# A 3x3 convolution plus residual: a rolled TensorE loop over four images, one weight load per four matmuls, hand-made semaphores, weights on another queue

## The chip, the cores and the metric

The kernel runs on one core of one Trainium2 chip. The metric is the device time of one execution in microseconds; lower is better. The four runs of the kernel before lie within 0.23 us (0.2%). "Span" is the length of the one profiled execution as the trace sees it; it is shorter than the time (123.3 us against 125.16 for the profiled run of the changed kernel).

## The reference

```python
batch, c_in, h, w, c_out, k = 16, 64, 64, 64, 64, 3      # all float32
x_pad = np.pad(x, ((0, 0), (0, 0), (1, 1), (1, 1)))
for b, co, ci, kh, kw in ...:
    output[b, co] += weight[co, ci, kh, kw] * x_pad[b, ci, kh:kh+h, kw:kw+w]
return output + residual
```

x, residual and output are 16.8 MB each, so at least 50.3 MB have to pass between HBM and the core; the page of the kernel before counts 33.70 MB read and 16.78 written.

## The kernel before

The images are taken in pairs: a pair of x is one 2 MB load over 128 partitions, and so are a pair of residuals and a pair of outputs. The chain of one image is: load x; cast it to bf16 and rearrange it so that even and odd rows lie on different partitions ("pack", on ScalarE, the first two images partly on VectorE); 24 matmuls of 512 or 504 columns into one of two PSUM tiles; two VectorE additions of the residual; after the second image of a pair, the store. All waits and semaphores are placed by the framework. The cuts are marked with dots.

```python
    xr = [pool.tile([128, NPIX], FP32, name=f"xr{i}") for i in range(NXR)]     # 3 raw pairs of x
    xp = [pool.tile([128, J + 1, W], BF16, name=f"xp{i}") for i in range(4)]   # 4 packed images
    ...
    def convolve(n):
        t = xp[n % 4]
        ps = psum.tile([128, NCHUNK, JC, W], FP32, name="ps")
        order = [(1, 0), (1, 1), (0, 0), (0, 1), (2, 0), (2, 1)]
        for i, (kw, d) in enumerate(order):
            ...
            for c in range(NCHUNK):                                            # 4 chunks
                nc.tensor.matmul(out=ps[:, c, :, xlo:xhi], lhsT=wl[:, d, kw, :, :]..., rhs=t[...], ...)
        return ps
    ...
    with tc.manual_schedule():
        nc.gpsimd.dma_start(out=wdup[:, 0, :], in_=w_flat[:, :])               # weights
        ...
        for p in range(NXR):
            load_x(p)
            load_ro(p)
        ...                                        # 9 transposes and 6 copies make wl
        pack(0)
        pack(1)
        for n in range(B):                         # written out: 16 x 24 matmuls, each with its load
            ps = convolve(n)
            if n + 2 < B:
                pack(n + 2)
            ...                                    # every second n: load_x, load_ro of a later pair
            add(n, ps)
            if n >= 9 and n % 2 == 1:
                store((n - 9) // 2)
        for p in range((B - 9) // 2 + 1, NPAIR):
            store(p)
```

Of the kernel before, what the change touches and what calls it, by code (L numbers as in the profile page):

```python
# [1 line left out]

# [5 lines left out]

FP32 = mybir.dt.float32
BF16 = mybir.dt.bfloat16  # L10
ADD = mybir.AluOpType.add


@with_exitstack
def kernel(
    ctx: ExitStack,
    tc: tile.TileContext,
    x: bass.AP,
    weight: bass.AP,
    residual: bass.AP,  # L20
    out: bass.AP,
):
    nc = tc.nc

    B, C, H, W = x.shape
    CO = weight.shape[0]
    K = weight.shape[2]
    assert C == 64 and CO == 64 and K == 3 and H == 64 and W == 64 and B == 16

    NPIX = H * W  # L30
    NPAIR = B // 2
    J = H // 2
    JC = 8
    NCHUNK = J // JC
    NXR = 3

    res_bc = residual.rearrange("b c h w -> (b c) (h w)")
    out_bc = out.rearrange("b c h w -> (b c) (h w)")
    x_bc = x.rearrange("b c h w -> (b c) (h w)")
    w_flat = weight.rearrange("co ci kh kw -> co (ci kh kw)")  # L40

    pool = ctx.enter_context(tc.tile_pool(name="pool", bufs=1))
    psum = ctx.enter_context(tc.tile_pool(name="psum", bufs=2, space=bass.MemoryType.PSUM))

    ident = pool.tile([64, 64], FP32)
    ro = [pool.tile([128, NPIX], FP32, name=f"ro{p}") for p in range(NPAIR)]
    xr = [pool.tile([128, NPIX], FP32, name=f"xr{i}") for i in range(NXR)]

    xp = [pool.tile([128, J + 1, W], BF16, name=f"xp{i}") for i in range(4)]

    wdup = ro[NPAIR - 1][0:64, 0:1152].rearrange("p (d f) -> p d f", d=2)
    wl = pool.tile([128, 2, 3, 2, 64], BF16)

    def load_x(p):
        nc.sync.dma_start(out=xr[p % NXR][:, :], in_=x_bc[128 * p : 128 * p + 128, :])

    def load_ro(p):
        nc.sync.dma_start(out=ro[p][:, :], in_=res_bc[128 * p : 128 * p + 128, :])

    def pack(n):  # L60

        p, im = divmod(n, 2)
        hp = slice(64 * im, 64 * im + 64)
        x4 = xr[p % NXR].rearrange("q (j two w) -> q j two w", two=2, w=W)
        t = xp[n % 4]
        first = nc.vector.tensor_copy if n < 2 else nc.scalar.copy
        first(out=t[64:128, 0:J, :], in_=x4[hp, :, 0, :])  # L67
        nc.scalar.copy(out=t[0:64, 1 : J + 1, :], in_=x4[hp, :, 1, :])  # L68

    def convolve(n):  # L70
        t = xp[n % 4]
        ps = psum.tile([128, NCHUNK, JC, W], FP32, name="ps")
        order = [(1, 0), (1, 1), (0, 0), (0, 1), (2, 0), (2, 1)]
        for i, (kw, d) in enumerate(order):
            xlo, xhi = max(0, 1 - kw), min(W, W + 1 - kw)
            for c in range(NCHUNK):
                j0 = JC * c
                nc.tensor.matmul(  # L78
                    out=ps[:, c, :, xlo:xhi],
                    lhsT=wl[:, d, kw, :, :].rearrange("q r c -> q (r c)"),  # L80
                    rhs=t[:, j0 + d : j0 + d + JC, xlo + kw - 1 : xhi + kw - 1],
                    start=i == 0,
                    stop=i == len(order) - 1,
                    skip_group_check=True,
                )
        return ps

    def add(n, ps):
        p, im = divmod(n, 2)
        hp = slice(64 * im, 64 * im + 64)  # L90
        o4 = ro[p].rearrange("q (j two w) -> q j two w", two=2, w=W)
        psj = ps.rearrange("q c j w -> q (c j) w")
        for par in range(2):
            nc.vector.tensor_tensor(  # L94
                out=o4[hp, :, par, :], in0=psj[64 * par : 64 * par + 64, :, :], in1=o4[hp, :, par, :], op=ADD
            )

    def store(p):
        nc.sync.dma_start(out=out_bc[128 * p : 128 * p + 128, :], in_=ro[p][:, :])


    with tc.manual_schedule():
        nc.gpsimd.dma_start(out=wdup[:, 0, :], in_=w_flat[:, :])  # L103
        make_identity(nc, ident[:, :])
        for p in range(NXR):
            load_x(p)
            load_ro(p)

        for t in xp:
            nc.vector.memset(t[0:64, 0, :], 0.0)  # L110
            nc.vector.memset(t[64:128, J, :], 0.0)  # L111
        nc.vector.memset(wl[0:64, 0, :, 1, :], 0.0)  # L112
        nc.vector.memset(wl[64:128, 1, :, 0, :], 0.0)  # L113


        nc.vector.tensor_copy(out=wdup[:, 1, :], in_=wdup[:, 0, :])  # L116
        wdup3 = wdup.rearrange("p d (ci t) -> p (d ci) t", t=9)
        tp = psum.tile([128, NCHUNK, JC, W], FP32, name="ps")
        for t in range(9):
            nc.tensor.transpose(out=tp[:, t // 8, t % 8, :], in_=wdup3[:, :, t], identity=ident[:, :])  # L120
        tpf = tp.rearrange("p c j w -> p (c j) w")
        for half, d, par, kh in (
            (0, 0, 0, 0),
            (1, 0, 0, 1),
            (1, 0, 1, 0),
            (0, 1, 0, 2),
            (0, 1, 1, 1),
            (1, 1, 1, 2),
        ):
            hp = slice(64 * half, 64 * half + 64)  # L130
            nc.vector.tensor_copy(out=wl[hp, d, :, par, :], in_=tpf[hp, 3 * kh : 3 * kh + 3, :])  # L131

        pack(0)
        pack(1)
        for n in range(B):
            ps = convolve(n)
            if n + 2 < B:
                pack(n + 2)
            p, im = divmod(n, 2)
            if im == 0 and p + NXR < NPAIR:  # L140
                load_x(p + NXR)
                load_ro(p + NXR)
            add(n, ps)
            if n >= 9 and n % 2 == 1:
                store((n - 9) // 2)
        for p in range((B - 9) // 2 + 1, NPAIR):
            store(p)


# [1 line left out]
_INS = ['x', 'weight', 'residual']  # L151
_OUTS = [((16, 64, 64, 64), 'float32')]


# [23 lines left out]
```

## Time and profile before

| | before |
|---|---|
| time, median (range) | 126.01 us (125.88 to 126.11) |
| span | 124.4 us |
| busy share TensorE / VectorE / ScalarE | 69% / 63% / 47% |
| bytes moved, mean rate | 50.53 MB, 406 GB/s |
| weight loads, TensorE | 393 of 99 to 205 ns, beside the matmuls |

The lines that carry the reading are in the prediction below. A transfer of 2 MB is cut into 128 packets of 16 KB, eight for each of the 16 DMA engines, and an engine that is late with one packet is late with all the later ones (in the kernel before, one that lost 1.57 us just after 40.23 us was still 1.56 us behind at the end). The packet records of the trace (start, duration, size, queue) show this; the aggregated views show it only at the very end of the span. The records don't name the DMA engine. Which packets belong to one engine is worked out: the next packet of an engine starts within some 10 ns of the end of the one before, and each engine closes its part of a transfer with a packet of 4 bytes.

### The profile page before, as it was taken

How to read it: one execution, taken by the hardware profiler on the slowest of the kernel's cores; microseconds unless marked ns; L12 is line 12 of the kernel's file. 1: busy time of each engine (PE TensorE's matmuls, PEld its weight loads, DVE VectorE, ACT ScalarE, POOL GpSimd, SP SyncE). 2: the span in 40 equal slices, each digit the busy share in tenths (PEclk: the TensorE clock that was granted, in tenths of full speed). 3: DMA queues.
4: the chain of work that ended last, by engine and by line, in shares of the span. 5: the costliest groups of instructions: out<-in, count | busy, mean ns of one | idle time of the engine just before them, and what ended most of it. 6: DMA issues, size and time to landing. Idle time of an engine off the chain costs nothing.

```text
span 124.4 us, 987 instructions
## 1 busy us (share of the span) xinstructions
PE 86.2 (69%) x386; PEld 39.2 (31%) x393; DVE 79.0 (63%) x51; ACT 58.2 (47%) x31; POOL 1.3 (1%) x7
## 2 busy tenths in 40 slices
PE   0004599999999999999999999999999900000000
PEld 0003134444444444444444444444444300000000
DVE  3015800989889898898988989889898894000000
ACT  4009207966984990896697599399000000000000
POOL 4000000000000000000000000000000000000000
PEclk9999999999999999999999999999999996555555
DMA  5999999999999999999999999999999999999980
GB/s 111 398 324 432 442 427 427 427 432 421 427 421 432 416 432 432 437 432 427 421 421 427 421 421 432 437 432 432 442 421 427 427 421 432 432 437 442 421 369 32
DMA packets 3507, 50.53 MB, mean 406 GB/s; under 512 B 400, under 2 KB 400, under 8 KB 432
## 3 DMA queue, kind: packets, MB, share of 16 engines
q1 hardware_dynamic: 3456, 50.33, 96.2%
q0 software_dynamic: 48, 0.15, 0.3%
q8 instruction: 3, 0.05, 0.2%
HBM read 33.70 MB, written 16.78 MB: 406 GB/s over the span
## 4 chain that ended last, share of the span: by engine, by line
PE 69%; DMA 6%; DVE 5%; DVEq 2%; issue 1%; POOLq 0%
PE ps L78 68%; DMA ro<-in_weight_dram 6%; DVEq L173 2%; DVE ro L94 2%; DVE wl L131 2%; PE ps L120 1%; DVE xp L67 1%; DVE ro L116 0%; POOLq L162 0%; POOLq masks.py:199 0%
## 5 line engine op out<-in xcount | busy, mean ns | idle before, releaser
L78 PE MATMUL ps<-xp,wl 128*128 128x504 bf16 (+1 forms) x377 | 85.0, 387 | 3.6 <-DVE xp L67 3.2
L94 DVE TENSOR_TENSOR ro<-ps,ro 64x2048 f32<-64x2048 f32 x32 | 73.2, 2289 | 15.5 <-PE ps L78 15.3
L78 PEld LDWEIGHTS <-wl 128*128 128x128 bf16 x384 | 38.0, 99 | 50.2 <-DVE xp L67 3.4
L67 ACT CAST xp<-xr 64x2048 bf16<-64x2048 f32 x14 | 26.5, 1896 | 20.6 <-DMA xr<-in_x_dram 20.4
L68 ACT CAST xp<-xr 64x2048 bf16<-64x2048 f32 x16 | 30.4, 1898 | 7.8 <-DMA xr<-in_x_dram 7.4
L120 PE MATMUL ps<-ident,ro 64*128 64x64 f32 x9 | 1.3, 319 | 9.4 <-DVE ro L116 9.4
L116 DVE COPY ro<-ro 64x576 f32<-64x576 f32 x1 | 0.5, 452 | 6.7 <-DMA ro<-in_weight_dram 6.7
L120 PEld LDWEIGHTS ps<-ident,ro 64*128 64x128 f32 x9 | 1.1, 205 | 9.4 <-issue 9.4
L131 DVE CAST wl<-ps 64x192 bf16<-64x192 f32 x6 | 2.0, 352 | 1.5 <-PE ps L120 1.4
L67 DVE CAST xp<-xr 64x2048 bf16<-64x2048 f32 x2 | 2.4, 1219 | 0.0
L68 ACT ACT_TABLE_LOAD x1 | 1.3, 1283 | 0.7 <-PEq L162 0.7
L110 DVE MEMSET xp<- 64x32 uint32 x4 | 0.3, 85 | 1.0 <-PEq L162 0.8
L103 POOL DMA_DIRECT2D ro<-in_weight_dram x1 | 0.6, 644 | 0.8 <-POOLq L162 0.8
L111 DVE MEMSET xp<- 64x32 uint32 x4 | 0.3, 85 | 0.2
masks.py:199 POOL TENSOR_SCALAR_AFFINE_SELECT ident<-ident 64x64 f32<-64x64 f32 x1 | 0.2, 228 | 0.1
L113 DVE MEMSET wl<- 64x96 uint32 x1 | 0.1, 138 | 0.1
L112 DVE MEMSET wl<- 64x96 uint32 x1 | 0.1, 138 | 0.1
masks.py:197 POOL MEMSET ident<- 64x64 f32 x1 | 0.2, 170 | 0.0
L162 POOL MEMSET const-bfloat16-1.0<- 128x1 bf16 x1 | 0.1, 112 | 0.0
L162 POOL MEMSET const-uint8-127<- 128x1 uint8 x1 | 0.1, 112 | 0.0
L162 POOL MEMSET const-float32-0.0<- 128x1 f32 x1 | 0.1, 109 | 0.2 <-issue 0.2
L162 POOL MEMSET const-float32-1.0<- 128x1 f32 x1 | 0.1, 110 | 0.0
## 6 DMA issues: line engine op xcount, KB each, us to landing
xr<-in_x_dram SPq DMA_DIRECT2D x8, 2048.0 KB, 23.1
ro<-in_residual_dram SPq DMA_DIRECT2D x8, 2048.0 KB, 27.6
out_dram<-ro SPq DMA_DIRECT2D x8, 2048.0 KB, 32.7
ro<-in_weight_dram POOLq DMA_DIRECT2D x1, 144.0 KB, 7.6
```

The lines of the kernel that those rows point to most:

```text
L67: first(out=t[64:128, 0:J, :], in_=x4[hp, :, 0, :])
L68: nc.scalar.copy(out=t[0:64, 1 : J + 1, :], in_=x4[hp, :, 1, :])
L78: nc.tensor.matmul(out=ps[:, c, :, xlo:xhi], lhsT=wl[:, d, kw, :, :].rearrange("q r c -> q (r c)"), rhs=t[:, j0 + d : j0 + d + JC, xlo + k ...
L94: nc.vector.tensor_tensor(out=o4[hp, :, par, :], in0=psj[64 * par : 64 * par + 64, :, :], in1=o4[hp, :, par, :], op=ADD)
L103: nc.gpsimd.dma_start(out=wdup[:, 0, :], in_=w_flat[:, :])
L110: nc.vector.memset(t[0:64, 0, :], 0.0)
L111: nc.vector.memset(t[64:128, J, :], 0.0)
L116: nc.vector.tensor_copy(out=wdup[:, 1, :], in_=wdup[:, 0, :])
L120: nc.tensor.transpose(out=tp[:, t // 8, t % 8, :], in_=wdup3[:, :, t], identity=ident[:, :])
L131: nc.vector.tensor_copy(out=wl[hp, d, :, par, :], in_=tpf[hp, 3 * kh : 3 * kh + 3, :])
L162: nc = _bacc.Bacc("TRN2", target_bir_lowering=False, num_devices=1)
L173: with _tile.TileContext(nc) as tc:
```

## The change

The intent is a leaner TensorE: a rolled loop over the four packed tiles in place of 16 written-out images, one weight load for each four matmuls that share weights, and semaphores chosen by hand in one critical section in place of those of the framework. The weights move from GpSimd's queue to ScalarE's ("ACT queue"), and all packs go to ScalarE. The last three stores stand after the section.

```diff
+    def matmul(out_, lhsT, rhs, start, stop, ldweights):
+        if ldweights:
+            return e.matmul(...)
+        return e.add_instruction(mybir.InstMatmult(..., ldweights=False))
...
+    with tc.tile_critical(no_gpsimd_drain=True):
+        for p in range(NPAIR):
+            if p >= NXR:
+                nc.sync.wait_ge(s_conv, 2 * (p - NXR) + 2)
+            load_x(p)
...
+        for p in range(NEARLY):                       # NEARLY = 5
+            nc.sync.wait_ge(s_add, 2 * p + 3)
+            store(p).then_inc(s_out, 16)
...
-        nc.gpsimd.dma_start(out=wdup[:, 0, :], in_=w_flat[:, :])
+        nc.scalar.dma_start(out=wdup[:, 0, :], in_=w_flat[:, :]).then_inc(s_w, 16)
...
+        with nc.Fori(0, B // NXP, 1, engines=[PE]):   # 4 turns of 4 images
+            for n in range(NXP):
+                nc.tensor.wait_ge(s_bank, 1).then_inc(s_bank, -1)
+                nc.tensor.wait_ge(s_pack, 1).then_inc(s_pack, -1)
+                for i, (kw, d) in enumerate(order):
+                    for c in range(NCHUNK):
+                        m = matmul(ps[n % 2]..., wl..., xp[n]..., i == 0, i == len(order) - 1, c == 0)
+                m.then_inc(s_conv, 1)
+    for p in range(NEARLY, NPAIR):
+        store(p)
```

More of the change, by code (lines that the diff above doesn't have):

```diff
@@ L6 @@
 from concourse._compat import with_exitstack
-from concourse.masks import make_identity
 FP32 = mybir.dt.float32
@@ L11 @@
 ADD = mybir.AluOpType.add
+PE = mybir.EngineType.PE
 @with_exitstack
@@ L35 @@
     NXR = 3
+    NXP = 4
+    NEARLY = 5
     res_bc = residual.rearrange("b c h w -> (b c) (h w)")
@@ L42 @@
     pool = ctx.enter_context(tc.tile_pool(name="pool", bufs=1))
-    psum = ctx.enter_context(tc.tile_pool(name="psum", bufs=2, space=bass.MemoryType.PSUM))
+    psum = ctx.enter_context(tc.tile_pool(name="psum", bufs=1, space=bass.MemoryType.PSUM))
     ident = pool.tile([64, 64], FP32)
@@ L47 @@
     xr = [pool.tile([128, NPIX], FP32, name=f"xr{i}") for i in range(NXR)]
-    xp = [pool.tile([128, J + 1, W], BF16, name=f"xp{i}") for i in range(4)]
+    xp = [pool.tile([128, J + 1, W], BF16, name=f"xp{i}") for i in range(NXP)]
     wdup = ro[NPAIR - 1][0:64, 0:1152].rearrange("p (d f) -> p d f", d=2)
     wl = pool.tile([128, 2, 3, 2, 64], BF16)
+    ps = [psum.tile([128, NCHUNK, JC, W], FP32, name=f"ps{i}") for i in range(2)]
+    sem = lambda name: tc.alloc_semaphore(name)
+    s_w = sem("s_w")
@@ L54, in load_x @@
+    s_x = [sem(f"s_x{p}") for p in range(NPAIR)]
+    s_r = [sem(f"s_r{p}") for p in range(NPAIR)]
+    s_out = sem("s_out")
+    s_id = sem("s_id")
+    s_wt = sem("s_wt")
+    s_pack = sem("s_pack")
+    s_bank = sem("s_bank")
+    s_conv = sem("s_conv")
+    s_add = sem("s_add")
     def load_x(p):
-        nc.sync.dma_start(out=xr[p % NXR][:, :], in_=x_bc[128 * p : 128 * p + 128, :])
+        nc.sync.dma_start(out=xr[p % NXR][:, :], in_=x_bc[128 * p : 128 * p + 128, :]).then_inc(s_x[p], 16)
@@ L57, in load_ro @@
     def load_ro(p):
-        nc.sync.dma_start(out=ro[p][:, :], in_=res_bc[128 * p : 128 * p + 128, :])
-    def pack(n):
-        p, im = divmod(n, 2)
-        hp = slice(64 * im, 64 * im + 64)
-        x4 = xr[p % NXR].rearrange("q (j two w) -> q j two w", two=2, w=W)
-        t = xp[n % 4]
-        first = nc.vector.tensor_copy if n < 2 else nc.scalar.copy
-        first(out=t[64:128, 0:J, :], in_=x4[hp, :, 0, :])
-        nc.scalar.copy(out=t[0:64, 1 : J + 1, :], in_=x4[hp, :, 1, :])
-    def convolve(n):
-        t = xp[n % 4]
-        ps = psum.tile([128, NCHUNK, JC, W], FP32, name="ps")
-        order = [(1, 0), (1, 1), (0, 0), (0, 1), (2, 0), (2, 1)]
-        for i, (kw, d) in enumerate(order):
-            xlo, xhi = max(0, 1 - kw), min(W, W + 1 - kw)
-            for c in range(NCHUNK):
-                j0 = JC * c
-                nc.tensor.matmul(
-                    out=ps[:, c, :, xlo:xhi],
-                    lhsT=wl[:, d, kw, :, :].rearrange("q r c -> q (r c)"),
-                    rhs=t[:, j0 + d : j0 + d + JC, xlo + kw - 1 : xhi + kw - 1],
-                    start=i == 0,
-                    stop=i == len(order) - 1,
-                    skip_group_check=True,
-                )
-        return ps
@@ L88, in add @@
-    def add(n, ps):
-        p, im = divmod(n, 2)
-        hp = slice(64 * im, 64 * im + 64)
-        o4 = ro[p].rearrange("q (j two w) -> q j two w", two=2, w=W)
-        psj = ps.rearrange("q c j w -> q (c j) w")
-        for par in range(2):
-            nc.vector.tensor_tensor(
-                out=o4[hp, :, par, :], in0=psj[64 * par : 64 * par + 64, :, :], in1=o4[hp, :, par, :], op=ADD
-            )
-    def store(p):
-        nc.sync.dma_start(out=out_bc[128 * p : 128 * p + 128, :], in_=ro[p][:, :])
@@ L102, with store @@
-    with tc.manual_schedule():
-        nc.gpsimd.dma_start(out=wdup[:, 0, :], in_=w_flat[:, :])
-        make_identity(nc, ident[:, :])
-        for p in range(NXR):
+        nc.sync.dma_start(out=ro[p][:, :], in_=res_bc[128 * p : 128 * p + 128, :]).then_inc(s_r[p], 16)
+    def store(p):
+        return nc.sync.dma_start(out=out_bc[128 * p : 128 * p + 128, :], in_=ro[p][:, :])
+    def matmul(out_, lhsT, rhs, start, stop, ldweights):
+        e = nc.tensor
+        if ldweights:
+            return e.matmul(out=out_, lhsT=lhsT, rhs=rhs, start=start, stop=stop, skip_group_check=True)
+        return e.add_instruction(
+            mybir.InstMatmult(
+                name=nc.get_next_instruction_name(),
+                engine=PE,
+                ins=[e.lower_ap(rhs), e.lower_ap(lhsT)],
+                outs=[e.lower_ap(out_)],
+                start_tensor_calc=start,
+                stop_tensor_calc=stop,
+                tile_size=(128, 128),
+                tile_position=(0, 0),
+                bass_skip_group_check=True,
+                ldweights=False,
+            )
+        )
@@ L106 @@
+    with tc.tile_critical(no_gpsimd_drain=True):
+        for p in range(NPAIR):
+            if p >= NXR:
+                nc.sync.wait_ge(s_conv, 2 * (p - NXR) + 2)
             load_x(p)
+            if p == NPAIR - 1:
+                nc.sync.wait_ge(s_wt, 2)
             load_ro(p)
+        for p in range(NEARLY):
+            nc.sync.wait_ge(s_add, 2 * p + 3)
+            store(p).then_inc(s_out, 16)
+        nc.gpsimd.memset(ident[:, :], 0.0).then_inc(s_id, 1)
+        nc.gpsimd.wait_ge(s_id, 1)
+        nc.gpsimd.affine_select(
+            out=ident[:, :],
+            in_=ident[:, :],
+            compare_op=mybir.AluOpType.not_equal,
+            fill=1.0,
+            base=0,
+            pattern=[[-1, 64]],
+            channel_multiplier=1,
+        ).then_inc(s_id, 1)
+        nc.scalar.dma_start(out=wdup[:, 0, :], in_=w_flat[:, :]).then_inc(s_w, 16)
+        for n in range(B):
+            p, im = divmod(n, 2)
+            hp = slice(64 * im, 64 * im + 64)
+            x4 = xr[p % NXR].rearrange("q (j two w) -> q j two w", two=2, w=W)
+            t = xp[n % NXP]
+            if im == 0:
+                nc.scalar.wait_ge(s_x[p], 16)
+            if n >= NXP:
+                nc.scalar.wait_ge(s_conv, n - NXP + 1)
+            nc.scalar.copy(out=t[64:128, 0:J, :], in_=x4[hp, :, 0, :])
+            nc.scalar.copy(out=t[0:64, 1 : J + 1, :], in_=x4[hp, :, 1, :]).then_inc(s_pack, 1)
@@ L113 @@
         nc.vector.memset(wl[64:128, 1, :, 0, :], 0.0)
-        nc.vector.tensor_copy(out=wdup[:, 1, :], in_=wdup[:, 0, :])
+        nc.vector.wait_ge(s_w, 16)
+        nc.vector.tensor_copy(out=wdup[:, 1, :], in_=wdup[:, 0, :]).then_inc(s_wt, 1)
+        nc.vector.wait_ge(s_wt, 2)
+        tpf = ps[0].rearrange("p c j w -> p (c j) w")
+        blocks = ((0, 0, 0, 0), (1, 0, 0, 1), (1, 0, 1, 0), (0, 1, 0, 2), (0, 1, 1, 1), (1, 1, 1, 2))
+        for half, d, par, kh in blocks:
+            hp = slice(64 * half, 64 * half + 64)
+            i = nc.vector.tensor_copy(out=wl[hp, d, :, par, :], in_=tpf[hp, 3 * kh : 3 * kh + 3, :])
@@ new lines @@
+        i.then_inc(s_bank, 2)
+        for n in range(B):
+            p, im = divmod(n, 2)
+            hp = slice(64 * im, 64 * im + 64)
+            o4 = ro[p].rearrange("q (j two w) -> q j two w", two=2, w=W)
+            psj = ps[n % 2].rearrange("q c j w -> q (c j) w")
+            if im == 0:
+                nc.vector.wait_ge(s_r[p], 16)
+            nc.vector.wait_ge(s_conv, n + 1)
+            for par in range(2):
+                i = nc.vector.tensor_tensor(
+                    out=o4[hp, :, par, :], in0=psj[64 * par : 64 * par + 64, :, :], in1=o4[hp, :, par, :], op=ADD
+                )
+                i.then_inc(s_add if par == 0 or n == B - 1 else s_bank, 1)
@@ L117 @@
+        nc.tensor.wait_ge(s_id, 2)
+        nc.tensor.wait_ge(s_wt, 1)
         wdup3 = wdup.rearrange("p d (ci t) -> p (d ci) t", t=9)
-        tp = psum.tile([128, NCHUNK, JC, W], FP32, name="ps")
         for t in range(9):
-            nc.tensor.transpose(out=tp[:, t // 8, t % 8, :], in_=wdup3[:, :, t], identity=ident[:, :])
-        tpf = tp.rearrange("p c j w -> p (c j) w")
-        for half, d, par, kh in (
-            (0, 0, 0, 0),
-            (1, 0, 0, 1),
-            (1, 0, 1, 0),
-            (0, 1, 0, 2),
-            (0, 1, 1, 1),
-            (1, 1, 1, 2),
-        ):
-            hp = slice(64 * half, 64 * half + 64)
-            nc.vector.tensor_copy(out=wl[hp, d, :, par, :], in_=tpf[hp, 3 * kh : 3 * kh + 3, :])
@@ L133 @@
-        pack(0)
-        pack(1)
-        for n in range(B):
-            ps = convolve(n)
-            if n + 2 < B:
-                pack(n + 2)
-            p, im = divmod(n, 2)
-            if im == 0 and p + NXR < NPAIR:
-                load_x(p + NXR)
-                load_ro(p + NXR)
-            add(n, ps)
-            if n >= 9 and n % 2 == 1:
-                store((n - 9) // 2)
-        for p in range((B - 9) // 2 + 1, NPAIR):
-            store(p)
+            i = nc.tensor.transpose(out=ps[0][:, t // 8, t % 8, :], in_=wdup3[:, :, t], identity=ident[:, :])
@@ new lines @@
+        i.then_inc(s_wt, 1)
+        with nc.Fori(0, B // NXP, 1, engines=[PE]):
+            for n in range(NXP):
+                nc.tensor.wait_ge(s_bank, 1).then_inc(s_bank, -1)
+                nc.tensor.wait_ge(s_pack, 1).then_inc(s_pack, -1)
+                order = [(1, 0), (1, 1), (0, 0), (0, 1), (2, 0), (2, 1)]
+                for i, (kw, d) in enumerate(order):
+                    xlo, xhi = max(0, 1 - kw), min(W, W + 1 - kw)
+                    for c in range(NCHUNK):
+                        j0 = JC * c
+                        m = matmul(
+                            ps[n % 2][:, c, :, xlo:xhi],
+                            wl[:, d, kw, :, :].rearrange("q r c -> q (r c)"),
+                            xp[n][:, j0 + d : j0 + d + JC, xlo + kw - 1 : xhi + kw - 1],
+                            i == 0,
+                            i == len(order) - 1,
+                            c == 0,
+                        )
+                m.then_inc(s_conv, 1)
@@ L151 @@
+    for p in range(NEARLY, NPAIR):
+        store(p)
+    with tc.tile_critical(sync_engine=mybir.EngineType.Pool, no_gpsimd_drain=True):
+        nc.gpsimd.wait_ge(s_out, 16 * NEARLY)
 _INS = ['x', 'weight', 'residual']
```

## The prediction

> **What bounds the kernel now.** I read the page's slices first, because busy shares of several engines are close together (PE 69%, DVE 63%).
>
> ```profile
> PE   0004599999999999999999999999999900000000
> ...
> DVE  3015800989889898898988989889898894000000
> ...
> DMA  5999999999999999999999999999999999999980
> GB/s 111 398 324 432 442 427 427 427 432 421 427 421 432 416 432 432 437 432 427 421 421 427 421 421 432 437 432 432 442 421 427 427 421 432 432 437 442 421 369 32
> ```
>
> TensorE looks like the bound between slices 5 and 32, but the DMA row is full from the second slice to the last but one, also where every compute engine is dark. 50.53 MB at the plateau of 427 GB/s take 118.3 us of the 124.4 us span. The page's chain that ended last gives PE 68%, but it only follows compute back from the final addition. The DMA queue's own waits show that after its last issue the program still sat on the stores:
>
> ```profile
> SPq L173 <- DMA out_dram<-ro: 18.7, 4, 4.8
> ```
>
> and the timeline near the end says how early the compute was done:
>
> ```profile
> 99.32 4.59 DVE L94 TENSOR_TENSOR ro<-ps,ro 64x2048 f32<-64x2048 f32 x2 [0.60 <-PE ps L78]
> 103.94 0.33 SPq L99 DMA_DIRECT2D out_dram<-ro  x1
> ```
>
> The last store is issued at 103.9 us; data flow until about 122.9. So some 17 us of transfers are queued when compute ends. Anything that only quickens TensorE, VectorE or ScalarE is worth nothing, as long as the queue never runs dry. What counts is the time of the first packet, what every packet costs, and when the last engine of the 16 is done.
>
> That last point is the one I followed further. Narrow windows (from:to, length, busy of PE, PEld, DVE, ACT, POOL with counts, PE clock, DMA share, GB/s) at the end:
>
> ```profile
> 118.00:119.00 1.00, 0.00 (x0) 0.00 (x0) 0.00 (x0) 0.00 (x0) 0.00 (x0) 0.50 1.03 442
> ...
> 120.00:121.00 1.00, 0.00 (x0) 0.00 (x0) 0.00 (x0) 0.00 (x0) 0.00 (x0) 0.50 0.80 344
> 121.00:122.00 1.00, 0.00 (x0) 0.00 (x0) 0.00 (x0) 0.00 (x0) 0.00 (x0) 0.50 0.20 82
> 122.00:123.00 1.00, 0.00 (x0) 0.00 (x0) 0.00 (x0) 0.00 (x0) 0.00 (x0) 0.50 0.08 33
> ```
>
> 82 and 33 GB/s are three of sixteen DMA engines and then fewer: thirteen stop at 120.8 to 121.3 us, three go on to 122.55, 122.79 and 122.90 (from the packet records in the trace). Each transfer is split evenly, eight 16 KB packets of 0.611 us on each engine, so an engine that loses time once stays behind to the end. In the same records the three fall behind one at a time, just after 40.2, 61.5 and 92.0 us. Three 16 KB packets of another queue start at exactly those times; the page counts them:
>
> ```profile
> q1 hardware_dynamic: 3456, 50.33, 96.2%
> q0 software_dynamic: 48, 0.15, 0.3%
> q8 instruction: 3, 0.05, 0.2%
> ```
>
> They are instruction fetches. The first took 1.10 us and stretched the data packet beside it from 0.611 to 1.08 us: 1.57 us lost on that engine, and the lag that remains (122.90 against 121.34) is 1.56.
>
> [...] The trace shows weights and x interleaved at 5.6 to 8.4 us. [...] The additions start every 5.185 us (21.52, 26.70, 31.89 us), and 24 matmuls in 5.185 us are 216 ns each, weight loads included. So the loads are hidden already. [...]
>
> **The change part by part.**
>
> *Weights once per four matmuls.* 288 of 384 weight loads go (99 ns each, beside a matmul). [...] All off the path.
>
> *The loop.* TensorE's program shrinks from 786 matmuls and loads plus some 20 waits, about 806 instructions[...], to 9 transposes with loads, 96 matmuls, 24 loads and about 20 others: some 160[...]. [...] I expect no fetch in mid-run, so the three laggards finish with the others: 122.90 - 121.34 = **1.56 us saved**. This is the only part that reaches the end.
>
> *Weights on the ACT queue.* GpSimd issues at 1.25 us, its packets start at 5.6, they land at 8.85. SP's first load gets its first packet 1.0 us after issue (0.75 to 1.76). An ACT issue near 1.0 us should therefore land at 4.5 to 6 us. From landing to the last weight copy takes 12.74 - 8.87 = 3.87 us now, so weights are ready at 8.5 to 10. Then x decides: it lands near 9.4; pack 0 is now two ScalarE casts of 1.90 instead of one ScalarE and one VectorE cast, 3.84 us with the gap; first convolution at 13.3 us instead of 13.93. Off the path. On the DMA engines the collision with weights stretched x packets by about 10 engine-us, 0.6 us on each engine, of which 147 KB at 427 GB/s are 0.35; if the hardware queue avoids the rest, up to 0.25 us. I book 0.1.
>
> *Own semaphores, critical section.* [...] x buffer p is refilled after both convolutions, not after both packs. Convolution 1 ends at 13.3 + 2.4 (the slow first microseconds, 85.4 - 16x5.185)[...] = 26 us, and six loads keep the DMA busy to 33. The last, x7, waits for convolution 9: 13.3 + 2.4[...] = 67.2 us, while 14 loads last to 72. Margin 5 us or more each time.
>
> *Last three stores after the section.* They now wait for all engines: convolutions end at 13.3 + 2.4[...] = 98.1, two additions of 2.29 give 102.7, exit handshake under 0.5: 103.2. Sixteen loads and five stores last until 106.2 on the earliest DMA engine[...].
>
> Sum: -1.56 - 0.1[...] = -1.5 us, **124.5 us**.
>
> **Rivals.** (1) *Nothing on the path changes*, 126.0 to 126.3: if fetches belong to another engine or the loop's branch causes them anew. For: the intervals 21.3 and 30.4 us are not equal[...]. Against: [...]no other engine has a hundred instructions. (2) *The queue runs dry before the last three stores.* [...] (3) *TensorE speedup pays*[...]. The 17 us backlog speaks against it.
>
> **Range and chances.** The laggards' repair is 1.56 or, if one fetch remains, about 0. Start and end costs are good for 0.5 us either way: 123.7 to 126.2. Faster by over 2% needs 123.49, a microsecond beyond all that I can name: 0.06. Slower by over 2% needs a dry queue: 0.04. Within: 0.90.
>
> **What would show it.** Instruction packets 3 to 0; the end windows fall from 442 to nothing within 0.6 us, with no 82 and 33; first convolution near 13.3, last addition done near 102.7; DMA full through 103 to 107. It is wrong if instruction packets remain, if a hole appears in the DMA row near 105, or if the first x packet starts later than 2.0 us.

The sum came to -1.5 us, 124.5 us, and one of its terms is cut: a loss at SP's start, for which I had nothing measured. The two terms that stand give -1.66 us. That the loop would leave nothing to fetch was my assumption from the length of the program (806 instructions against some 160); no trace of the kernel before shows how long a program may be. In the steps for x7 and for the last stores the time per image is cut, as I had guessed it a little below the 5.185 us measured; with 5.185 convolution 1 would end at 26.1 us, x7 wait until 67.6, and the convolutions end at 98.7 and the additions at 103.2. The exit, "under 0.5", took 0.29 us in the changed kernel (103.44 to 103.73).

## The result

| | before | after |
|---|---|---|
| time, median (range) | 125.99 us (125.88 to 126.11), 4 runs | 125.13 us (124.81 to 125.20), 4 runs |
| ratio | | 0.9927 (95%: 0.9907 to 0.9946) |
| span | 124.4 us | 123.3 us |

A ratio is the mean time of one kernel's fast runs over that of the other's of the same rounds, so it is not quite the ratio of the medians beside it. The change saves 0.9 us.

The page after. First the slices (busy tenths in 40 slices of the span) and the DMA queues (packets, MB, share of 16 engines' span):

```profile
DMA  4999999999999999999999999999999999999992
GB/s 90 378 360 430 425 425 430 430 430 436 430 430 425 430 430 425 436 430 425 425 425 425 430 425 425 425 425 436 436 430 436 441 430 425 436 430 425 425 430 85
...
q1 hardware_dynamic: 3456, 50.33, 96.8%
q10 hardware_dynamic: 80, 0.15, 0.3%
```

The DMA row is as full as before, and the plateau is the same 425 to 441 GB/s. The row of instruction packets is gone; the weights are now 80 packets of the ACT queue (q10) instead of 48 of GpSimd's. The last slice carries 85 GB/s in place of 32: the transfers run at full width closer to the end of the span. The narrow windows (from:to, length, busy of five engines, PE clock, DMA share, GB/s) show it:

```profile
118.00:119.00 1.00, 0.00 (x0) 0.00 (x0) 0.00 (x0) 0.00 (x0) 0.00 (x0) 0.50 1.03 442
...
120.00:121.00 1.00, 0.00 (x0) 0.00 (x0) 0.00 (x0) 0.00 (x0) 0.00 (x0) 0.50 0.73 311
121.00:122.00 1.00, 0.00 (x0) 0.00 (x0) 0.00 (x0) 0.00 (x0) 0.00 (x0) 0.50 0.04 16
122.00:123.00 1.00, 0.00 (x0) 0.00 (x0) 0.00 (x0) 0.00 (x0) 0.00 (x0) 0.50 0.00 0
```

Where before had 82 and 33 GB/s there are 16 and 0. Compute ends when it did, to half a microsecond; this is the end of the timeline (start, length, instruction):

```profile
98.83 4.61 DVE L163 TENSOR_TENSOR ro<-ps,ro 64x2048 f32<-64x2048 f32 x2 [0.51 <-PE ps L83]
103.73 1.58 SPq L76 DMA_DIRECT2D out_dram<-ro  x3
```

and this the DMA queue's own wait at the end, 16.8 us in place of 18.7:

```profile
SPq L225 <- DMA out_dram<-ro: 16.8, 3, 7.1
```

So the program still sits on queued stores for some 17 us after the last store was issued. The gain is not TensorE's: 288 fewer weight loads left the rhythm of the additions where it was (four images from 36.59 to 57.34 us, 5.187 us each; before 5.185).

The packet records, as completion times on the 16 DMA engines of the last 2 MB store, say where the gain lies:

```
                 first 13 engines     last three engines        mid-run instruction packets (start us)
before           120.79 .. 121.35     122.56  122.80  122.91    40.23  61.53  91.97
after            120.60 .. 121.29     121.32  121.56  121.70    none
```

The first thirteen engines end at the same time in both kernels. In the kernel before only the three that carried an instruction packet ended later. In the changed kernel no engine is that late; the last one is 0.4 us behind the thirteen (more on this below).

### The profile page after: what moved, and what is told of

It is laid out like the page before. It is cut to its first block, busy times and chain, and to the rows that moved or that the text cites. A ratio compares the mean times of both kernels' runs of the same rounds, so it can differ in the third digit from the quotient of the medians.

```text
span 123.3 us, 730 instructions
## 1 busy us (share of the span) xinstructions
PE 85.9 (70%) x389; PEld 10.6 (9%) x105; DVE 76.6 (62%) x49; ACT 62.0 (50%) x33; POOL 0.6 (0%) x6
## 4 chain that ended last, share of the span: by engine, by line
PE 69%; DVEq 2%; DVE 2%; issue 0%
PE ps L83 52%; PE ps L82 17%; DVEq L98 2%; DVE ro L163 2%
## 5 line engine op out<-in xcount | busy, mean ns | idle before, releaser
L83 PE MATMUL ps<-xp,wl 128*128 128x504 bf16 (+1 forms) x288 | 79.3, 385 | 0.2
L135 ACT CAST xp<-xr 64x2048 bf16<-64x2048 f32 x16 | 30.3, 1896 | 22.3 <-DMA xr<-in_x_dram 22.1
L82 PE MATMUL ps<-xp,wl 128*128 128x504 bf16 (+1 forms) x92 | 35.5, 385 | 2.4 <-PEq L179 2.4
L136 ACT CAST xp<-xr 64x2048 bf16<-64x2048 f32 x16 | 30.4, 1897 | 0.2
L82 PEld LDWEIGHTS ps<-xp,wl 128*128 128x128 bf16 x96 | 9.5, 99 | 76.8 <-issue 76.8
```

Source lines behind the costliest of these rows:

```text
L82: return e.matmul(out=out_, lhsT=lhsT, rhs=rhs, start=start, stop=stop, skip_group_check=True)
L83: return e.add_instruction(mybir.InstMatmult(name=nc.get_next_instruction_name(), engine=PE, ins=[e.lower_ap(rhs), e.lower_ap(lhsT)], outs ...
L135: nc.scalar.copy(out=t[64:128, 0:J, :], in_=x4[hp, :, 0, :])
L136: nc.scalar.copy(out=t[0:64, 1 : J + 1, :], in_=x4[hp, :, 1, :]).then_inc(s_pack, 1)
```

## The experiments

The theory: TensorE's program of some 800 instructions in "before" is fetched while it runs, in the three instruction packets of 16 KB that the page counts; each is one packet on one DMA engine, in a stream that has no slack (DMA share 0.98 to 1.03 in the windows of the kernel before from 14 to 120 us); this engine ends late, and the end of the kernel is the end of the last engine. The loop makes the program so short that nothing is fetched in mid-run (no instruction packet in the changed kernel's page). The rivals: fewer weight loads or fewer waits on TensorE gave the gain; the move of the weights to another queue gave it. All ten variants are correct and were timed with five rounds beside the kernel before on the same chip.

**The loop written out.**

```diff
-        with nc.Fori(0, B // NXP, 1, engines=[PE]):
+        for _turn in range(B // NXP):
```

> The changed kernel with its TensorE loop written out: same semaphores, same four-per-load weights, only the program is longer (393 matmuls, 105 weight loads and about 45 others, some 540 instructions). Fetch theory: one or two instruction packets of 16 KB return, each puts one DMA engine 1.57 us behind, so the last data packet ends near 121.3 + 1.57 = 122.9 us instead of 121.7 and the time is 125.1 + 1.2 = 126.3 us, ratio to before 1.00 to 1.003. TensorE or semaphore theory (the gain is from fewer weight loads or fewer waits): no change against the changed kernel, 125.1 us, ratio 0.993.

Measured: 126.06 us against 126.10 before, ratio 1.0009 (0.9987 to 1.0030). The whole gain is gone, though the weight loads are still 96, and semaphores, section and queues are as changed. The page and the windows of this run:

```profile
q8 instruction: 1, 0.02, 0.1%
```

```profile
121.00:122.00 1.00, 0.00 (x0) 0.00 (x0) 0.00 (x0) 0.00 (x0) 0.00 (x0) 0.50 0.08 33
122.00:123.00 1.00, 0.00 (x0) 0.00 (x0) 0.00 (x0) 0.00 (x0) 0.00 (x0) 0.50 0.04 16
```

One packet is back (at 50.96 us, 1.06 us long; a second starts only at 124.42 us, after the span), and one engine streams on alone after 122 us. In the packet records a transfer takes about 4.9 us on an engine; on the engine that carries the fetch this one takes 6.43 us (47.92 to 54.34): 1.5 us lost. A data packet ends at 50.97, the fetch follows at once, and the next data packet runs from 52.01 to 53.12, 1.11 us instead of 0.611. The last data end at 122.62 us, 0.9 us later than in the changed kernel. This is the main evidence: the work and its order are the same, and only the loop is written out.

**Loop kept, a weight load for every matmul.**

```diff
-                            c == 0,
+                            True,
```

> The changed kernel, loop kept, weights loaded for every matmul again (about 230 instructions[...]). Fetch theory: no instruction packet, no laggard, 125.1 us (ratio 0.993), additions every 5.18 us instead of 5.11 and the last one about 1 us later, which the queued transfers hide. TensorE theory: the gain of the change is given back, 126.0 us, ratio 1.000.

Measured: 125.95 us, ratio 1.0000 (0.9979 to 1.0021). My expectation missed: I had counted about 230 instructions and no fetch. Taken alone, the time would favour the TensorE theory. But the page has the packet back:

```profile
q8 instruction: 1, 0.02, 0.1%
...
L82 PE MATMUL ps<-xp,wl 128*128 128x504 bf16 (+1 forms) x384 | 85.6, 387 | 2.4 <-PEq L179 2.4
L82 PEld LDWEIGHTS ps<-xp,wl 128*128 128x128 bf16 x384 | 37.6, 99 | 50.1 <-issue 9.5
```

It starts at 57.75 us, its engine ends at 122.67 us, and thirteen of the others end by 121.31. The additions keep the rhythm of the changed kernel (36.59 to 57.34 there, 37.27 to 58.02 here, both 20.75 us for four images), so the 288 extra loads cost TensorE nothing that the additions see. So a program of about 230 instructions was not short enough. Why it fetched, and why only once and near the third turn of the loop, I did not settle.

**A weight load for every second matmul.** This is the case that the run before had spoiled: more loads, no fetch.

```diff
-                            c == 0,
+                            c % 2 == 0,
```

> The changed kernel, loop kept, weights loaded for every second matmul: 192 loads in place of 96, about 180 TensorE instructions. The variant with 384 loads had grown to about 230 and fetched one block. Fetch theory: no instruction packet at 180, so the time is that of the changed kernel, ratio 0.991 to 0.995, last addition within 0.3 us. TensorE theory (weight loads cost time): a third of the way back to before, ratio 0.995 to 0.997, without any instruction packet.

Measured: 125.07 us, ratio 0.9927 (0.9909 to 0.9946); the unaltered changed kernel of the same rounds had 0.9919 (0.9903 to 0.9935). No instruction packet in the page, last data at 121.67 us. The number of loads

```profile
L82 PEld LDWEIGHTS ps<-xp,wl 128*128 128x128 bf16 x192 | 19.1, 99 | 68.5 <-issue 68.5
```

is twice that of the changed kernel, and the time is the same within 0.13 us. Weight loads are worth nothing here.

**Both: written out, and a load for every matmul.** TensorE's program is then as long as in the kernel before, everything else as changed.

> The changed kernel with its loop written out and weights loaded for every matmul: TensorE's program is as long as in the kernel before (some 820 instructions), all else as changed. Fetch theory: three instruction packets as in before, on three different DMA engines; since only the last engine counts, the time is that with one fetch, 125.9 to 126.4 us, ratio 0.999 to 1.003, last data packet at 122.6 to 123.0 us. If fetches added up on one engine: 128 us or more. TensorE theory (semaphores and section gave the gain): 125.0 us.

Measured: 125.98 us, ratio 0.9992 (0.9975 to 1.0008). The page counts three fetches as in the kernel before,

```profile
q8 instruction: 3, 0.05, 0.2%
```

at 34.6, 70.8 and 102.7 us, and three engines end late, at 122.20, 122.27 and 122.27 us, against 121.40 at most for the other thirteen. Three fetches cost as much as one (126.06 us above), because they fall on three engines and only the last engine counts. The last data end at 122.27, a little before the 122.6 that I expected.

**Fetches by another engine.** The changed kernel plus 600 memsets of one column on GpSimd, which is idle; nothing reads them.

```diff
+        for _k in range(600):
+            nc.gpsimd.memset(scratch[:, _k : _k + 1], 0.0)
```

> The changed kernel plus 600 one-column memsets on the idle GpSimd into a scratch tile that nobody reads: TensorE, VectorE, ScalarE and all data transfers untouched[...]. Fetch theory: two or three instruction packets appear in GpSimd's name, each with one DMA engine 1.57 us behind if they come after the transfers have started, and the time is 126.3 us, about that of before. If all fetches of one engine's program use one DMA engine, the lag adds up to 3 us or more: 128 us. TensorE theory: 125.1 us, no change.

Measured: 129.00 us, ratio 1.0228 (1.0205 to 1.0252), 4 us above the changed kernel. GpSimd's timeline and the page's queue row:

```profile
8.07 4.28 POOL L125 MEMSET scratch<- 128x1 f32 x128 [0.53 <-issue]
13.46 4.28 POOL L125 MEMSET scratch<- 128x1 f32 x128 [1.10 <-issue]
18.40 4.28 POOL L125 MEMSET scratch<- 128x1 f32 x128 [0.66 <-issue]
```

```profile
q14 instruction: 5, 0.04, 0.1%
```

GpSimd runs 182, 128, 128, 128 and 34 memsets and is idle for 0.53 to 1.10 us between them. The packets are five of 8 KB, at 6.3, 11.8, 16.8, 21.7 and 26.7 us; each of the first four starts some 0.6 to 1.2 us before such a pause, which fits a wait for the next instructions, though the trace names no releaser. They all fall on the same DMA engine. This is read from one engine's lag: its distance to the second slowest grows by steps, 0.06, 0.70, 1.36, 2.01 and 2.67 us over the first five transfers, and then stays between 2.5 and 2.7 us to the end, where it streams alone:

```profile
123.00:124.00 1.00, 0.00 (x0) 0.00 (x0) 0.00 (x0) 0.00 (x0) 0.00 (x0) 0.50 0.08 33
...
125.00:126.00 1.00, 0.00 (x0) 0.00 (x0) 0.00 (x0) 0.00 (x0) 0.00 (x0) 0.50 0.04 16
```

So the instruction fetches of an otherwise idle engine made one DMA engine late, and the kernel with it. Of the 4.4 us by which the last data came later than in the changed kernel (126.05 against 121.70) this lag explains about 2.6. The other engines also ended later than there (the second slowest at 123.50): their packets were slow between 80 and 84 us, when loads give way to stores, by 17 us summed over 16 engines, 1.1 us each. I did not find out why, and this part stays open. Nor did the filler leave the other engines untouched, as I had expected: VectorE's copy of the weights took 2.84 us instead of 0.45 while the memsets ran, and the last stores were issued 2.9 us later (106.58 against 103.73). That is not what made the last DMA engine late: it was busy with an earlier transfer until 111.46 us.

**The weights, three ways.** First the changed kernel with the weights on GpSimd again.

```diff
-        nc.scalar.dma_start(out=wdup[:, 0, :], in_=w_flat[:, :]).then_inc(s_w, 16)
+        nc.gpsimd.dma_start(out=wdup[:, 0, :], in_=w_flat[:, :]).then_inc(s_w, 16)
```

> The changed kernel with the weights issued from GpSimd again. Fetch theory: no instruction packet, time within 0.2 us of the changed kernel, 124.9 to 125.3 us. Weight-queue theory (part of the 0.9 us came from moving the weights): 0.4 us or more slower, 125.5 to 126 us. It also shows whether the sixteenth DMA engine, which started 0.9 us after the others in the changed kernel (first packet at 3.17 us, others 1.96 to 2.23), starts late because of the ACT queue: if so its lag of 0.25 us at the end disappears and the time is 124.9 us.

Measured: 125.28 us, ratio 0.9940 (0.9922 to 0.9958). No instruction packet, last data at 121.90 us. The gain stays. The slowest engine is as late after the first transfer as it is with the ACT queue (9.34 us against 9.22; 0.40 us behind the middle of the group against 0.47), so a lag of this size appears without the ACT queue too. Then the reverse, the kernel before with this one line changed.

> The kernel before with one line changed: weights on the ACT queue. Fetch theory: three instruction packets, three laggards, 125.8 to 126.2 us, ratio 0.998 to 1.002. Weight-queue theory: 125.1 to 125.5 us.

Measured: 126.19 us, ratio 1.0004 (0.9985 to 1.0022), three instruction packets, three engines late (122.17 to 122.77). Moving the weights gives nothing. Last, the changed kernel with the weights on SP, ahead of the first x.

```diff
+        nc.sync.dma_start(out=wdup[:, 0, :], in_=w_flat[:, :]).then_inc(s_w, 16)
         for p in range(NPAIR):
```

> The changed kernel with the weights issued on SP ahead of the first x load, so that they no longer alternate with x packets. Fetch theory: the 147 KB have to pass anyway, 0.37 us of each DMA engine; if they fall into the slow first microsecond, the last data packet comes up to 0.4 us earlier, 124.7 to 125.1 us; weights land before 5 us in place of 9.7 and the first convolution starts at 13.3 or as soon as x is packed, which the end doesn't feel. Theory that early weights matter: over 1 us faster, below 124 us.

Measured: 124.70 us (124.64 to 124.92), ratio 0.9904 (0.9885 to 0.9922). It is the fastest median, 0.24 us below the changed kernel of the same rounds, but the intervals overlap. The timeline of the start:

```profile
3.86 0.45 DVE L145 COPY ro<-ro 64x576 f32<-64x576 f32 x1 [1.46 <-DMA ro<-in_weight_dram]
...
13.41 0.59 PE L82 MATMUL ps<-xp,wl 128*128 128x512 bf16 x1 [7.69 <-PEq L179]
```

The weights land 5.8 us earlier than with the ACT queue, and the first convolution starts only 0.5 us earlier, because x decides; the end gains 0.2. The last data come at 121.30 us, and the last engine is 0.1 us behind the next.

**All stores inside the section, and the changed kernel once more.**

```diff
-    NEARLY = 5
+    NEARLY = 8
```

> The changed kernel with all eight stores inside the section, each waiting only for its own additions, so that the last three no longer wait for all engines to leave it. Fetch theory: the queue never ran dry there (stores issued at 103.7 us, data queued until 106), so no change beyond 0.2 us, 124.9 to 125.3 us. If the handshake costs time: 0.3 to 1 us faster, 124.1 to 124.8.

Measured: 125.30 us, ratio 0.9944 (0.9927 to 0.9960), last data at 121.57 us. The three late stores cost nothing where they stand; nothing is gained by moving them, and the median is 0.36 us above the changed kernel's. The data transfers do not show this, but the end of the program does: from the last data to the end of the span it takes 1.99 us, against 1.53 in the run that follows.

> The changed kernel unaltered, timed beside the variants of this set on one chip. Fetch theory: no instruction packet before the last data packet, last data packet at 121.5 to 121.8 us, ratio to before 0.991 to 0.995. If its ratio came out at 1.00 the first result would have been chance.

Measured: 124.94 us (124.84 to 125.05), ratio 0.9919 (0.9903 to 0.9935), no instruction packet, last data at 121.50 us. The first result is confirmed.

Fetches in mid-run against the time, for all kernels in which TensorE's program or the weights differ:

```
kernel                              weight loads   fetches   last data us   ratio
before                                  384           3         122.91      1
before, weights on ACT queue            384           3         122.77      1.0004
changed, written out, all loads         384           3         122.27      0.9992
changed, all loads                      384           1         122.67      1.0000
changed, written out                     96           1         122.62      1.0009
changed, every second load              192           0         121.67      0.9927
changed, weights on GpSimd               96           0         121.90      0.9940
changed                                  96           0         121.50      0.9919
changed, weights first on SP             96           0         121.30      0.9904
```

Every kernel with a fetch is at 0.999 to 1.001, every one without at 0.990 to 0.994. Weight loads and weight queue do not sort them. The packet records sort the kernels in the same way: after the first 10 us, each of the eleven fetches in this table is followed by one data packet of 0.98 to 1.11 us, the engine has lost 1.3 to 1.6 us, and no other data packet of 16 KB in these kernels takes longer than 0.67 us.

## Why the prediction was right

The time predicted was 124.5 us; 125.13 and 124.94 were measured, inside the range of 123.7 to 126.2. That alone says little, since the kernel before, at 125.99, lies in this range too, and the saving was 0.86 us where 1.5 were forecast. What was right is the mechanism, as the packet counts and the experiments show. By its own steps:

- *The bound.* Right. The DMA engines are full from the first loads to the end in both kernels, compute ends 18 us before the last data, and more weight loads at an equal number of fetches did not move the time by more than 0.1% (192 against 96 loads without a fetch: 0.9927 and 0.9919; 384 against 96 loads with one fetch: 1.0000 and 1.0009).
- *The loop.* Right in mechanism: instruction packets went from 3 to 0, and the last data from 122.91 to 121.70 us. The fetches of the kernel before cost DMA engines time and TensorE none that shows: the additions kept 5.18 us across the one at 40.23 us (37.08 to 42.26). The term was 1.56 us; the last data came 1.21 us earlier in the first profile and 1.41 in the second (121.50), net of all other terms. The end windows were to fall to nothing within 0.6 us; from the first engine's end to the last's it took 1.1 (120.60 to 121.70). What I had overlooked: I took for granted that all sixteen engines would end as the thirteen of before. In the changed kernel one engine is already the last by 0.25 us after the very first transfer (9.22 us against 8.97 for the next), and this lag stays; near the end a second engine has fallen behind as well (121.56). Such a lag after the first transfer is there in all of the changed kernel's variants in the table, in differing size (0.06 to 0.25 us to the next engine; 0.13 with the weights first on SP), and in the kernel before it is 0.03. Its cause was not isolated.
- *Rival 1* had in its favour that the fetches were not evenly spaced (21.3 and 30.4 us apart). They are TensorE's nevertheless: writing out its loop brought one back, and writing out the loop with all loads brought three. *Rivals 2 and 3* did not come about: the last addition ended at 103.44 us, before any DMA engine was done with the earlier transfers (106.01), and TensorE's loads did not move the time (0.9927 with 192, 0.9919 with 96).
- *Weights once per four matmuls.* Nothing on the path, as said, and nothing off it: 5.187 us per image against 5.185.
- *Weights on the ACT queue.* The step "should land at 4.5 to 6 us" was wrong. They landed at 9.69 us, 0.8 us later than from GpSimd before. The ACT queue issued them at 0.91 us, but their first packet started at 5.0, 4.1 us later. By then SP had handed over its six loads (the last issue ends at 4.03 us), which fits weights that wait for these, but no run isolates it. Then on each DMA engine its four packets of 2.3 KB and one end packet took turns with the 16 KB packets of x. I had carried SP's 1.0 us for the first transfer (0.75 to 1.76) over to a second queue. The first convolution stayed at 13.93 us instead of 13.3: the weights were ready only at 13.58, and pack 0 ended later still, at 13.67, because x had landed near 9.9 and not at 9.4. As the step was off the path, it cost nothing, and the 0.1 us booked for it did not show.
- *Section and semaphores.* SP's first issue moved from 0.75 to 0.95 us, the first data packet from 1.76 to 1.96: 0.20 us lost. What cost it was not isolated. The refills came when forecast (x7 issued at 67.70 us against 67.2) and the queue never ran dry.
- *Last three stores.* Last addition done at 103.44 us (102.7 forecast), stores issued from 103.73, 0.29 us later. The earliest engine was done with the earlier transfers at 106.0, 2.3 us after the first of these issues, and the queue did not run dry (377 to 475 GB/s in each microsecond from 103 to 108).
- *A term that was missing.* From the last data to the end of the span it takes 1.65 us here (121.70 to 123.34) instead of 1.50 (122.91 to 124.41). I had not looked at the end block. The difference is no proven part of the change: the same kernel took 1.53 us when it was run again, and the kernel before with the weights on the ACT queue took 1.67.

Summed for the first profile: 1.21 saved at the last data, 0.14 given back in the end block, 1.07 us of the span; between the medians of the time, 0.86.

## What to carry to other kernels

When a kernel is bound by transfers as this one was, ask when the last of the DMA engines ends and not what their mean does; one or two microseconds at the end with a tenth or a fifth of the bandwidth (here 82 and 33 of 442 GB/s) can be a sign that single engines were held up somewhere. A long unrolled program was itself traffic here (three packets of 16 KB, each 1.3 to 1.6 us of one DMA engine): a loop that left nothing to fetch in mid-run took 0.9 us off, and its matmul savings took nothing. Count the instruction packets in the profile rather than trust a count of instructions: some 160 fetched nothing here, and some 230 fetched once. Before crediting such a gain to the operation that was rewritten, write the loop out again and see whether the gain stays.
